# The third projection group of a Fourier branch: both differences taken ahead of the last shift on VectorE, both sums by accumulating transfers

## The chip, the core and the metric

The kernel runs on one core of a Trainium2 chip. The core has five engines, each of which runs its own list of instructions strictly in order: TensorE (PE, matmuls; PEld is its weight load), VectorE (DVE), ScalarE (ACT), GpSimd (POOL) and SyncE (SP), which here only issues transfers. Transfers between device memory and the on-chip memory run on 16 DMA engines; GpSimd, ScalarE and SyncE can each issue them, and a transfer that adds to what is in the on-chip memory is issued by GpSimd here. Engines wait for each other by semaphores. The metric is the time of one execution on the device in microseconds (us).

## The reference, cut to what matters

The model has two layers over 256 tokens of `x` and 256 of `ctx`, all in float32. Layer 0 is a Fourier branch; the change lies in its first half:

```python
shift, scale, gate = split(silu(c) @ ada_w + ada_b, 3)
h = rmsnorm(x, g) * (1 + scale) + shift
u, z = split(h @ w_in, 2)                  # w_in: 2048 x 8192, u: 256 x 4096
ug = u.reshape(b, n, 16, 256)              # 16 groups of 256 channels
f = fft2(ug, axes=(tokens, channels), norm='ortho').real
f = einsum('bngc,gcd->bngd', f, w_mix)     # one 256 x 256 mix per group
x = x + gate * ((f * silu(z)) @ w_out)
```

The same is done for `ctx` with its own shift and scale. Layer 1 is an attention branch, and a last norm ends the model.

## The kernel before, in words

The kernel takes the transform over tokens first: it multiplies the normed inputs by a cosine and sine matrix (the DFT units), so that what is projected, `hx`, is already transformed: 16 blocks (k) of 128 features, each with 256 positions for `x` and 256 for `ctx`. Scale acts on all positions, the shift only on position 0. The transform over channels is then folded into the weights: of a group's 256 columns of `w_in`, columns c and 256 - c enter as their difference (called m) and their sum (called p); the two columns that have no partner (0 and 128) of all groups form one small special product (`asp`). So each group needs, of its weight columns, one difference and one sum for each half (kh = 0, 1) of the 2048 features.

Every float32 product is made of three matmuls: an operand is split into a high part, rounded by ScalarE (line 60), and a low part, subtracted by VectorE (line 61); TensorE runs high x high, high x low and low x high (lines 73 to 75).

The work goes through these stages. (1) An opening of 16 steps (`opening_step`): SyncE loads weights of scale and shift (`ada_tile`), TensorE multiplies them, ScalarE copies the rows (`ada_rows`), TensorE turns them and VectorE reduces them (`ada_fin`, lines 222 to 225). Then `scale_hx` scales four blocks of `hx` into high and low parts (lines 276 and 277), and `fix_f0` adds the shift to their position 0 (lines 229 to 235). Steps alternate: scale of four blocks, then shift of the same four; the last `ada_fin` and `fix_f0(3)`, behind the loop, are the last shift. Projection matmuls of groups 0 and 1 fill TensorE between (`fill_pe`). (2) The other groups, g = 2 to 15: for each group TensorE runs the m product (48 matmuls, both halves), the mix of the group before (`mix`, 14 matmuls, ends in VectorE's sums `ft`, lines 504 and 505, which GpSimd writes out, line 509), the p product (48), and `load_m`'s product that turns the next mix weights into `pqh`, `pql` and `sp` (10). (3) The z part, the output product and layer 1.

A group's weights come in two loads of 1016 KB, one for each half, into the pool `raw` of three buffers (line 34), issued by SyncE (line 46). `fold_uh` makes of each the difference (line 122, into a tile `wm` of the pool `ws`) and, for g of 2 or more, the sum in place in the raw buffer: for half 0 by VectorE (line 128), for half 1 by a transfer that GpSimd issues (line 131), which fetches the second columns again from device memory and adds them to the first ones there. It has to wait until the difference is taken, since it overwrites an operand. `split_uh` makes high and low parts of both (`wmh`, `wml`, `wph`, `wpl`), into a pool of eight tiles; the raw buffer is free when `wpl` is made.

A planner puts the instructions of each engine into one order, by its own estimate of when each can run. `tc.issue_after(x)` adds that the instructions within, as far as they are on the same engine as x, stand behind x in that order. In the kernel before, group 2's folding and splitting stands within such a block in the loop over g (lines 432 to 437): half 0 behind the last shift (`f0_end`), half 1 behind the low part of the special product (`asp_end`). Its loads stand in SyncE's queue behind the last weights of the opening.

Of the kernel before, what the change touches and what calls it, by code (L numbers as in the profile page):

```python
# [10 lines left out]
F32 = mybir.dt.float32  # L11
F32R = mybir.dt.float32r
AF = mybir.ActivationFunctionType
ALU = mybir.AluOpType
# [14 lines left out]
def tile_dit(ctx: ExitStack, tc: tile.TileContext, a: dict, out: bass.AP):  # L29
    nc = tc.nc  # L30
    V, S, PE, GP = nc.vector, nc.scalar, nc.tensor, nc.gpsimd
# [70 lines left out]
    gs0 = const.tile([P, KT, 2], F32, name="gs0")  # L102
# [11 lines left out]
    GP.memset(c32, 0.0)  # L114
    V.tensor_copy(c32[:, :, 0:2], cc)

    def load_uh(g, kh, ld=raw, *until):
        return ld(a["wu"][g, kh], *until)[:, : 8 * 2 * 127].rearrange("p (k s c) -> p k s c", k=8, s=2)

    def fold_uh(v, g, kh):  # L120
        m = wsp.tile([P, 8, 127], F32, tag="ws", name="wm")
        V.tensor_tensor(m, v[:, :, 0, :], v[:, :, 1, :], op=ALU.subtract)
        if g < 2:
            t = wsp.tile([P, 8, 127], F32, tag="ws", name="wp")
            V.tensor_tensor(t, v[:, :, 0, :], v[:, :, 1, :], op=ALU.add)
            return t, m
        if kh == 0:
            V.tensor_tensor(v[:, :, 0, :], v[:, :, 0, :], v[:, :, 1, :], op=ALU.add)
        else:
            b = a["wu"][g, kh].rearrange("p (k s c) -> p k s c", k=8, s=2)[:, :, 1, :]  # L130
            nc.gpsimd.dma_start(out=v[:, :, 0, :], in_=b, accum_op=ALU.add)
        return v[:, :, 0, :], m

    def split_uh(v, m):
        fl = {}
        for nm, t in (("m", m), ("p", v)):
            l = wfp.tile([P, 8, 127], F32R, tag="wf", name=f"w{nm}l")
            h = wfp.tile([P, 8, 127], F32R, tag="wf", name=f"w{nm}h")
            split(h, l, t)
            fl[nm] = (h, l)  # L140
        return fl
# [14 lines left out]
    with tc.tile_pool(name="st", reuse_waits="tile", bufs=1, side="right") as st:  # L156
# [40 lines left out]
        f0_end = [None]  # L197
# [16 lines left out]
        def ada_fin(nb, which, rows):  # L214
            o2 = psum()
            with pe_next():
                for j in range(4):
                    r = PE.transpose(o2[:, j * P : (j + 1) * P], rows[:, j * P : (j + 1) * P], ident)
            pe_end[0] = r.ins
            kq = slice(nb * 4, nb * 4 + 4)  # L220
            dst = (sh0, gs0)[which][:, kq, :]
            V.tensor_reduce(dst, o2.rearrange("p (a j s) -> p a s j", a=4, j=4)[:, :, 0:2, :], axis=AX.X, op=ALU.add)
            V.tensor_tensor(dst, dst, adab[:, 0, which, kq], op=ALU.add)
            if which:
                V.scalar_tensor_tensor(dst, dst, 1.0, ng[:, 0, kq], op0=ALU.add, op1=ALU.mult)
# [38 lines left out]
        def evac_dft(k):  # L264
# [3 lines left out]
            V.tensor_copy(f0[:, k, :], o[:, 0::N])  # L268
            hx.append(r)

        def scale_hx(k):
            r = hx[k]
            h, l = act(F32R), act(F32R)
            for s in range(2):
                q = slice(s * N, (s + 1) * N)
                S.activation(h[:, q], r[:, q], AF.Copy, scale=gs0[:, k, s : s + 1])
                V.scalar_tensor_tensor(l[:, q], r[:, q], gs0[:, k, s : s + 1], h[:, q].bitcast(F32), op0=ALU.mult, op1=ALU.subtract)
            hx[k] = (h.rearrange("p (s j) -> p s j", s=2), l.rearrange("p (s j) -> p s j", s=2))

        raws, pend = {}, []  # L280
# [116 lines left out]
        for p in range(8, 16):  # L397
# [18 lines left out]
            for kh, q in ((0, 9), (1, 11)):  # L416
                if p == q:
                    raws[kh, 1] = fold_uh(raws[kh, 1], kh, 1)
                if p == q + 1:
                    with tc.issue_after(rows_end[0]):  # L420
                        wu[kh][1] = split_uh(*raws[kh, 1])
        ada_fin(*pend.pop())
        fix_f0(3)
        fill_pe(len(fill))

# [4 lines left out]
    asp = up.tile([96, 2, 130], F32R, name="asp", bufs=1)  # L430
    for g in range(G):
        if g == 2:
            v = [load_uh(g, kh) for kh in range(2)]
            w = []
            for kh in range(2):
                with tc.issue_after((f0_end[0], asp_end)[kh]):
                    w.append(split_uh(*fold_uh(v[kh], g, kh)))
        else:
            w = load_u(g) if g > 1 else wu[g]
        if g == 0:  # L440
# [33 lines left out]
        if g == 0:  # L474
# [4 lines left out]
            asp_end = V.tensor_tensor(asp[32:64], ov, asp[0:32].bitcast(F32), op=ALU.subtract).ins  # L479
# [73 lines left out]
    with tc.tile_pool(name="yp", reuse_waits="tile", bufs=32) as ypool:  # L553
# [20 lines left out]
        with tc.tile_pool(name="zp", reuse_waits="tile", bufs=2) as zp:  # L574
# [10 lines left out]
            for kg in range(4):  # L585
                wr = raw(a["wz0"][kg])
                w = []
# [5 lines left out]
                for j in range(4):  # L593
                    k = kg * 4 + j
                    wh, wl = w[j // 2]
                    for b in range(4):
                        q = slice((j % 2) * 512 + b * P, (j % 2) * 512 + (b + 1) * P)
# [6 lines left out]
            for b in range(4, NB):  # L604
                w = ws_split(raw(a["wz"][b - 4]))
# [3 lines left out]
                for k in range(KT):  # L609
                    wh, wl = w[k // 8]  # L610
                    q = slice((k % 8) * P, (k % 8 + 1) * P)
# [29 lines left out]
        for i in range(32):  # L641
# [3 lines left out]
            w = ws_split(raw(a["wo0"][sw, kg]))  # L645
# [10 lines left out]
            for j, b in [(j, b) for b in range(8) for j in range(2)] if edge else [(j, b) for j in range(2) for b in range(8)]:  # L656
                q = slice(b * P, (b + 1) * P)
# [53 lines left out]
    with tc.tile_pool(name="h1", reuse_waits="tile", bufs=16) as h1p:  # L711
        hx1 = []
        v2 = [[None] * 2 for _ in range(4)]
        kT = []
        with tc.tile_pool(name="kvp", reuse_waits="tile", bufs=2) as kvp:
            hc1 = []
            for k in range(KT):
# [3 lines left out]
                for s, h in ((0, hx), (1, hc)):  # L721
                    q = slice(s * N, (s + 1) * N)
# [6 lines left out]
            for kg in range(8):  # L729
                w = ws_split(raw(a["wkv"][kg]))  # L730
                for j in range(2):
                    k = kg * 2 + j
                    wh, wl = w[j]
                    for tb in range(4):
                        h = (hx1, hc1)[tb // 2][k]
                        c = (tb % 2) * P
                        for kv in range(2):
                            q = slice(kv * 512, (kv + 1) * 512)
# [276 lines left out]
        with tc.tile_pool(name="fin", reuse_waits="tile", bufs=1) as fp:  # L1015
# [22 lines left out]
            for k in range(12, NB, 2):  # L1038
                w = w1_next()
# [5 lines left out]
            for kg in range(16):  # L1045
                w = ws_split(raw(a["wo1b"][kg]))
                for j in range(2):
                    k = kg * 2 + j
                    wh, wl = w[j]
                    for tb in range(2):  # L1050
                        for c in range(2):
                            q = slice(c * 512, (c + 1) * 512)
# [24 lines left out]
            for kg in range(8):  # L1077
                t = raw(a["wo1c"][kg])
                if kg < 5:
                    w = [(h[:, q], l[:, q]) for h, l in ws_split(t) for q in (slice(0, 512), slice(512, 1024))]  # L1080
                else:
                    w = []
# [123 lines left out]
```

## Time and profile before

| what | us |
|---|---|
| median of three runs | 1873.78 |
| lowest and highest run | 1867.76, 1873.89 |
| the profiled execution, its own time | 1867.94 |
| its span | 1865.8 |
| TensorE busy in the span | 1817.2 |
| VectorE busy | 1390.8 |
| ScalarE busy | 953.4 |
| GpSimd busy | 175.2 |

Granted TensorE clock over the span: 0.996 of full speed. Times in the timelines count from the start of the span. The last scaling of the opening ends at 112.5 us, the last shift starts at 117.0 us, and the groups from 2 on run to about 330 us.

How to read the rows: a row of a timeline has start, duration, engine, line, operation, output and inputs by the program's names (numbers left out), shapes and count; brackets at the end give the idle time of the engine before it and what ended it. A row of the waits has who waited for whom, the total, the number of times and the longest. A row of busy time by stretch has the stretch, its length, the busy time of each engine with its instructions, the granted clock (1.00 is full), the share of DMA time and GB/s. Groups have a count, the busy time and the mean duration in ns, and the idle time before them. A `q` behind an engine's name is its instruction queue, which issues transfers.

### The profile page before, as it was taken

The numbers are of one execution on the slowest core, as the hardware profiler recorded it, in microseconds if no ns is written. First come the engines' busy times: TensorE is split into PE (matmuls) and PEld (weight loads), VectorE is DVE, ScalarE is ACT, GpSimd is POOL, SyncE is SP. The second block draws the span as 40 slices with busy tenths as digits, with TensorE's granted clock in tenths as the row PEclk, the third lists the DMA queues.
The fourth block names the chain that finished last, engine by engine and source line by source line (L and its number), as shares of the span: only waits on it lengthen the run. The fifth ranks groups of instructions, "written<-read, shape, count | busy, mean of one in ns | idle before, by whom it ended". The sixth has DMA issues, their size and how long they took to land.

```text
span 1865.8 us, 26461 instructions
## 1 busy us (share of the span) xinstructions
PE 1817.2 (97%) x9889; PEld 1548.6 (83%) x9889; DVE 1390.8 (75%) x2767; ACT 953.4 (51%) x1657; POOL 175.2 (9%) x188
## 2 busy tenths in 40 slices
PE   6889999999999999999999999999999999999997
PEld 4569999888888888888888787888888888887886
DVE  4658888787868788687983835788878878887455
ACT  5534444432222243324231624888888888896343
POOL 0001111200000000000000001112220220300001
PEclk9999999999999999999999999999999999999999
DMA  9978888656566547754576323333333333434543
GB/s 396 416 252 227 229 241 244 249 203 247 209 248 230 205 166 280 270 215 147 214 279 227 118 90 136 136 136 114 135 113 136 124 125 136 158 136 175 188 179 135
DMA packets 75087, 366.87 MB, mean 197 GB/s; under 512 B 22160, under 2 KB 22304, under 8 KB 39888
## 3 DMA queue, kind: packets, MB, share of 16 engines
q1 hardware_dynamic: 49104, 324.83, 47.2%
q0 software_dynamic: 21280, 32.63, 6.9%
q10 hardware_dynamic: 4576, 7.74, 1.3%
q8 instruction: 77, 1.26, 0.3%
q14 instruction: 50, 0.41, 0.1%
HBM read 352.58 MB, written 12.59 MB: 196 GB/s over the span
## 4 chain that ended last, share of the span: by engine, by line
PE 84%; DMA 7%; DVE 4%; issue 2%; ACT 2%; POOL 0%; ACTq 0%; POOLq 0%; DVEq 0%
PE ps L74 21%; PE ps L73 21%; PE ps L75 21%; PE ps L905 6%; PE ps L907 3%; DMA raw<-in_wu 3%; PE ps L961 3%; DMA raw<-in_awp 3%; PE ps L976 2%; PE ps L975 2%; PE ps L941 2%; PE ps L942 1%; PE ps L206 1%; DVE wpl L61 1%; DMA dm<-in_dmat 0%
## 5 line engine op out<-in xcount | busy, mean ns | idle before, releaser
L60 ACT CAST wh<-raw 128x1024 fp32r<-128x1024 f32 x333 | 349.5, 1051 | 556.7 <-PE ps L74 491.0
L61 DVE TENSOR_TENSOR wl<-raw,wh 128x1024 fp32r<-128x1024 f32 x333 | 421.1, 1267 | 261.1 <-ACT wh L60 258.9
L74 PE MATMUL ps<-act,wh 128*128 128x512 f32 x1024 | 398.2, 389 | 0.0
L73 PE MATMUL ps<-act,wh 128*128 128x512 f32 x1024 | 393.7, 389 | 0.0
L75 PE MATMUL ps<-act,wl 128*128 128x512 f32 x1024 | 391.2, 389 | 0.0
L75 PEld LDWEIGHTS ps<-act,wl 128*128 128x128 f32 x1024 | 192.3, 188 | 39.9
L74 PEld LDWEIGHTS ps<-act,wh 128*128 128x128 f32 x1024 | 192.3, 188 | 39.8
L73 PEld LDWEIGHTS ps<-act,wh 128*128 128x128 f32 x1024 | 192.3, 188 | 39.7
L905 PE MATMUL ps<-h,wh 128*128 128x512 f32 x512 | 186.8, 400 | 0.0
L540 DVE CUSTOM_DVE_ANT_0 raw<-raw,cb 128x512 f32<-128x512 f32 x256 | 172.4, 687 | 15.2 <-DMA raw<-in_adw 11.1
L540 DVE CUSTOM_DVE_ANT_0 junk<-raw,cb 128x512 f32<-128x512 f32 x192 | 131.6, 685 | 11.9 <-ACT cb L532 8.4
L907 PE MATMUL ps<-h,wl 128*128 128x256 f32 x512 | 138.1, 280 | 0.0
L74 PE MATMUL ps<-wl,h 128*128 128x512 f32 x320 | 125.6, 392 | 1.5 <-DVE wl L61 1.5
L73 PE MATMUL ps<-wh,h 128*128 128x512 f32 x320 | 124.4, 397 | 0.2 <-ACT h L724 0.2
L75 PE MATMUL ps<-wh,h 128*128 128x512 f32 x320 | 124.4, 391 | 0.0
L905 PEld LDWEIGHTS ps<-h,wh 128*128 128x128 f32 x512 | 96.1, 188 | 18.8
L943 DVE CUSTOM_DVE_ANT_0 ps<-ps,mask,nsink 128x512 f32<-128x512 f32 x128 | 92.0, 753 | 11.9 <-PE ps L942 10.8
L946 ACT ACTIVATE p<-ps,mx 128x512 f32<-128x512 f32 x128 | 87.2, 687 | 24.7 <-DVE mx L943 24.1
L907 PEld LDWEIGHTS ps<-h,wl 128*128 128x128 f32 x512 | 96.8, 189 | 1.4
L61 DVE TENSOR_TENSOR pl<-ps,ph 128x512 fp32r<-128x512 f32 x128 | 83.6, 684 | 10.0 <-ACT ph L60 9.1
L951 ACT ACTIVATE p<-p,sm 128x512 f32<-128x512 f32 x128 | 85.4, 716 | 7.8 <-DVE sm L949 7.8
L74 PE MATMUL ps<-wl,ys 128*128 128x512 f32 x212 | 83.3, 393 | 0.0
(311 smaller groups left out, 3565.8 us busy)
## 6 DMA issues: line engine op xcount, KB each, us to landing
raw<-in_wz SPq DMA_DIRECT2D x64, 1024.0 KB, 4.9
raw<-in_adw SPq DMA_DIRECT2D x64, 1024.0 KB, 4.9
raw<-in_awp SPq DMA_DIRECT2D x32, 1024.0 KB, 13.6
raw<-in_wo SPq DMA_DIRECT2D x32, 1024.0 KB, 5.5
raw<-in_wq SPq DMA_DIRECT2D x32, 1024.0 KB, 4.9
raw<-in_wu SPq DMA_DIRECT2D x32, 1016.0 KB, 7.3
raw<-in_wo1b SPq DMA_DIRECT2D x16, 1024.0 KB, 4.8
act<-in_xT POOLq DMA_DIRECT2D x32, 256.0 KB, 5.4
```

The source lines that it names most:

```text
L60: S.copy(h, src)
L61: V.tensor_tensor(l, src, h.bitcast(F32), op=ALU.subtract)
L73: PE.matmul(o, wh, xh, start=start, stop=False)
L74: PE.matmul(o, wh, xl, start=False, stop=False)
L75: return PE.matmul(o, wl, xh, start=False, stop=stop).ins
L540: V.tensor_tensor_reduce(junk if s == 0 and i < 3 else wf, wf, cb[:, s, kq * 512 : kq * 512 + 512], 1.0, 0.0, ALU.mult, ALU.add, acc[:, i, ...
L905: PE.matmul(o[0], wh[:, q], hx1[k], start=k == 0, stop=k == KT - 1)
L907: PE.matmul(o[0][:, 0:N], wl[:, q], hx1[k][:, 0:N], start=False, stop=False)
L943: V.tensor_tensor_reduce(o, o, mask[:, tb, :], -0.125, nsink[:, i : i + 1], ALU.add, ALU.min, mx[:, tb : tb + 1])
L946: S.activation(pt[:, tb, :], so[tb], AF.Exp, bias=mx[:, tb : tb + 1], scale=-1.0, accum_out=sm[:, tb : tb + 1])
L951: S.activation(pt[:, tb, :], pt[:, tb, :], AF.Copy, scale=sm[:, tb : tb + 1])
L961: PE.transpose(o[:, (kt * 2 + tb) * P : (kt * 2 + tb + 1) * P], pt[:, tb, c : c + P], ident)
```

## The change

Group 2's loads and foldings move from the loop over g to the end of the opening. Both differences stand behind the last scaling in VectorE's order (`scale_end`), and the last `ada_fin`, with it the last shift, stands behind the second difference (`fold_end`). Both sums of group 2 are now made by accumulating transfers that GpSimd issues; from group 3 on half 0 is summed by VectorE as before. The splits of both halves stand behind the last shift, and the order behind the special product's low part is no longer asked for.

```diff
     def fold_uh(v, g, kh):
         m = wsp.tile([P, 8, 127], F32, tag="ws", name="wm")
-        V.tensor_tensor(m, v[:, :, 0, :], v[:, :, 1, :], op=ALU.subtract)
+        fold_end[0] = V.tensor_tensor(m, v[:, :, 0, :], v[:, :, 1, :], op=ALU.subtract).ins
...
-        if kh == 0:
+        if kh == 0 and g > 2:
             V.tensor_tensor(v[:, :, 0, :], v[:, :, 0, :], v[:, :, 1, :], op=ALU.add)
         else:
             b = a["wu"][g, kh].rearrange("p (k s c) -> p k s c", k=8, s=2)[:, :, 1, :]
...
-                V.scalar_tensor_tensor(l[:, q], r[:, q], gs0[:, k, s : s + 1], h[:, q].bitcast(F32), op0=ALU.mult, op1=ALU.subtract)
+                scale_end[0] = V.scalar_tensor_tensor(l[:, q], r[:, q], gs0[:, k, s : s + 1], h[:, q].bitcast(F32), op0=ALU.mult, op1=ALU.subtract).ins
...
-        ada_fin(*pend.pop())
+        v2 = [load_uh(2, kh) for kh in range(2)]
+        with tc.issue_after(scale_end[0]):
+            v2 = [fold_uh(v2[kh], 2, kh) for kh in range(2)]
+        with tc.issue_after(fold_end[0]):
+            ada_fin(*pend.pop())
         fix_f0(3)
         fill_pe(len(fill))
...
         if g == 2:
-            v = [load_uh(g, kh) for kh in range(2)]
-            w = []
-            for kh in range(2):
-                with tc.issue_after((f0_end[0], asp_end)[kh]):
-                    w.append(split_uh(*fold_uh(v[kh], g, kh)))
+            with tc.issue_after(f0_end[0]):
+                w = [split_uh(*f) for f in v2]
```

The planner's order changes with it. On VectorE the two differences stand right behind the last scaling; behind the shift follow the low first difference, the special product, the low first sum, and, ahead of group 1's mix weights and of group 3's first difference, the low second difference. On ScalarE the rounding of the first difference stands ahead of the copy of the last rows, and the rounding of the first sum ahead of that of the second difference. On GpSimd one issue more stands ahead of the writes of group 0. On TensorE eight of the ten matmuls of group 3's mix weights move into the p product of group 2; the planner's order differs in a like manner in several of the groups that follow. SyncE's order is the same.

More of the change, by code (lines that the diff above doesn't have):

```diff
@@ L115, in tile_dit @@
     V.tensor_copy(c32[:, :, 0:2], cc)
+    fold_end = [None]
     def load_uh(g, kh, ld=raw, *until):
@@ L269, in evac_dft @@
             hx.append(r)
+        scale_end = [None]
         def scale_hx(k):
```

## The prediction

> **What bounds the kernel now.** I read the page first (span, busy time, the chain), then busy time by stretch, then who TensorE waits for in the projection, then the timelines of TensorE and VectorE around the longest of those waits.
>
> ```profile
> span 1865.8 us, 26461 instructions
> PE 1817.2 (97%) x9889; PEld 1548.6 (83%) x9889; DVE 1390.8 (75%) x2767; ACT 953.4 (51%) x1657; POOL 175.2 (9%) x188
> PE 84%; DMA 7%; DVE 4%; issue 2%; ACT 2%; POOL 0%; ACTq 0%; POOLq 0%; DVEq 0%
> ```
>
> TensorE is the bound: 97% busy, 84% of the chain. A change elsewhere is worth what it takes out of TensorE's waits, at most 3% of the span, so I look for the waits near the edit.
>
> ```profile
> core 0: us, PE busy (x) PEld busy (x) DVE busy (x) ACT busy (x) POOL busy (x), PEclk, DMA share, GB/s
> 116.00:130.00 14.00, 12.96 (x107) 12.25 (x105) 12.83 (x30) 7.60 (x15) 1.51 (x1) 1.00 0.35 105
> 130.00:140.00 10.00, 7.25 (x48) 7.26 (x49) 7.43 (x11) 4.42 (x9) 1.14 (x2) 0.83 0.82 212
> 140.00:185.00 45.00, 42.79 (x353) 42.38 (x353) 37.84 (x57) 19.84 (x39) 9.28 (x10) 1.00 0.86 226
> 185.00:230.00 45.00, 44.19 (x363) 43.65 (x362) 37.86 (x55) 20.43 (x40) 7.77 (x9) 1.00 0.83 231
> 230.00:315.00 85.00, 85.00 (x707) 85.00 (x707) 74.21 (x107) 38.09 (x76) 15.08 (x18) 1.00 0.87 238
> ```
>
> The edit lies at 112 to 140 us. Before 130 VectorE is full (12.83 of 14 us); at 130 to 140 TensorE has its hole and a granted clock of 0.83; from 230 TensorE never stops, one matmul per 85.00/707 = 0.120 us. Its waits from 118 to 340 us:
>
> ```profile
> PE ps L75 <- DVE wml L61: 4.6, 2, 3.5
> PE ps L74 <- DVE apl L61: 1.9, 3, 1.1
> PE ps L499 <- DVE asp L479: 0.3, 1, 0.3
> ```
>
> The longest, 3.5 us, is for the low part of group 2's second difference. On TensorE's timeline:
>
> ```profile
> 129.00 0.28 PE L74 MATMUL ps<-act,wmh 128*127 128x256 f32 x1
> 132.75 0.52 PE L75 MATMUL ps<-act,wml 128*127 128x256 f32 x1 [3.46 <-DVE wml L61]
> ...
> 135.84 0.41 PE L74 MATMUL ps<-act,wmh 128*127 128x256 f32 x1
> ...
> 136.97 0.28 PE L73 MATMUL ps<-mh,ch 128*128 128x256 f32 x1
> ```
>
> From 129.00 to 136.97 lie 23 matmul steps: 23 x 0.120 = 2.76 us of work in 7.97, so 5.2 us lost: 3.46 waiting, the rest at the slow clock after it (132.75 to 135.84 is 15 steps of 0.206). That is the prize. VectorE at the same place:
>
> ```profile
> 116.95 0.19 DVE L222 TENSOR_REDUCE sh<-ps 128x8 f32<-128x32 f32 x1 [4.48 <-PE ps L218]
> ...
> 118.69 0.41 DVE L347 TENSOR_TENSOR mt<-m 128x256 f32<-128x256 f32 x1
> 119.03 1.21 DVE L122 TENSOR_TENSOR wm<-raw 128x1016 f32<-128x1016 f32 x1
> ...
> 121.42 1.21 DVE L128 TENSOR_TENSOR raw<-raw 128x1016 f32<-128x1016 f32 x1
> ...
> 124.12 0.42 DVE L479 TENSOR_TENSOR asp<-ps,asp 32x260 fp32r<-32x260 f32 x1
> 124.57 1.22 DVE L122 TENSOR_TENSOR wm<-raw 128x1016 f32<-128x1016 f32 x1
> ...
> 127.84 1.20 DVE L61 TENSOR_TENSOR wpl<-raw,wph 128x1016 fp32r<-128x1016 f32 x1
> ...
> 131.49 1.20 DVE L61 TENSOR_TENSOR wml<-wm,wmh 128x1016 fp32r<-128x1016 f32 x1
> ...
> 136.98 1.22 DVE L61 TENSOR_TENSOR wpl<-raw,wph 128x1016 fp32r<-128x1016 f32 x1 [2.56 <-ACT wph L60]
> ```
>
> VectorE idles 4.48 us ahead of the last shift, then runs both differences of group 2 (119.03, 124.57) and one sum (121.42) when it is late already; the awaited low part comes at 131.49.
>
> **The change, part by part.**
>
> *Two differences ahead of the shift.* They follow the last scaling, which ends 4.48 us before 116.95, at 112.47: 112.5 to 114.9 with 2 x 1.21. Cover: the idle time, 2.1 us of which stay. If it went (a late load), the shift would slip by as much. The second half's load:
>
> ```profile
> 106.59 0.33 SPq L46 DMA_DIRECT2D raw<-in_wu  x1
> ```
> ```profile
> raw<-in_wu SPq DMA_DIRECT2D x1, 1016.0 KB, 6.9
> ```
>
> It lands at 113.5; its subtraction starts at 113.7. Cost nothing. ScalarE's rounding of the first difference (about 1.05 us) now stands ahead of its copy of the last rows:
>
> ```profile
> 114.94 0.59 ACT L211 COPY rows<-ps 128x512 f32<-128x512 f32 x1 [3.00 <-PE ps L206]
> 123.19 1.06 ACT L60 CAST wph<-raw 128x1016 fp32r<-128x1016 f32 x1
> 126.01 1.05 ACT L60 CAST wmh<-wm 128x1016 fp32r<-128x1016 f32 x1
> ```
>
> From 113.7 it ends at 114.8, before the copy's 114.94: no cost, with 0.1 us to spare.
>
> *One sum off VectorE.* With the differences, 3 x 1.21 = 3.6 us leave VectorE between 118.7 and 131.5. The low part of the special row (124.12) no longer stands behind a difference and a sum, so TensorE's 0.3 us wait for it goes. The program's order also puts group 2's second low difference ahead of group 1's mix weights and group 3's first difference.
>
> *Two accumulating transfers on GpSimd.* This is the new wait: ScalarE's rounding of the first sum now follows a landing, and behind it in ScalarE's order stand a rounding for group 1, a copy for the mix and the rounding of the second difference; on VectorE, behind the low part of that sum, stand one subtraction, two output sums and the low second difference. The rows of before:
>
> ```profile
> 126.37 1.51 POOL L131 DMA_DIRECT2D raw<-in_wu  x1 [13.63 <-PE ps L75]
> ```
> ```profile
> L131 POOL DMA_DIRECT2D raw<-in_wu x14: 1478/1488/1513, 126.4 to 314.0; - x14
> ...
>   ACT wph L60: 43.1, 12
> ...
> DMA to landing us min/median/max: 8.1/12.6/13.4
> ```
> ```profile
> 135.91 1.04 ACT L60 CAST wph<-raw 128x1016 fp32r<-128x1016 f32 x1 [4.08 <-DMA raw<-in_wu]
> ```
>
> The issue at 126.37 came 0.6 us after the subtraction it waits for (124.57 + 1.22); its sum was used at 135.91, 9.5 us on. So the first sum is issued at 114.3 and lands at T0 = 122.4 to 127.7 by the shortest and longest of the fourteen. I take 9.5, T0 = 123.8, the landing nearest in time and the first of its queue after a pause, as this one is. When is it due? Prices on VectorE:
>
> ```profile
> L61 DVE TENSOR_TENSOR wpl<-raw,wph 128x1016 fp32r<-128x1016 f32 x27 | 32.7, 1210 | 5.8 <-ACT wph L60 5.8
> ...
> L504 DVE TENSOR_TENSOR ft<-ps,gsb 128x256 f32<-128x256 f32 x26 | 10.8, 414 | 0.0
> L505 DVE TENSOR_TENSOR ft<-ps,gsb 128x254 f32<-128x254 f32 x26 | 10.6, 409 | 0.0
> ...
> L122 DVE TENSOR_TENSOR wm<-raw 128x1016 f32<-128x1016 f32 x28 | 34.0, 1216 | 20.8 <-DMA raw<-in_wu 20.7
> ...
> L61 DVE TENSOR_TENSOR apl<-ps,aph 127x260 fp32r<-127x260 f32 x14 | 5.9, 420 | 0.0
> ```
>
> From T0 to the low second difference: 1.06 + 1.21 + 0.42 + 0.41 + 0.41 + 1.20 = 4.7 us. TensorE wants it one step after 129.00, less the 0.3 gained: 128.8. So T0 is due at 124.1; 123.8 leaves 0.3 us. Each us later costs one.
>
> The second sum is issued 1.5 us behind the first, in the same queue. Bounds: 115.8 + 8.1 = 123.9 if nothing shares, 123.8 + 9.5 = 133.3 if it runs only after the first; I take 115.8 + 12.6 = 128.4, the median of the fourteen, as this one shares the engines with the first. Behind it on ScalarE stand a small copy and the rounding of group 3's mix weights (0.6, like the rows' copy of that size), some 1.7 us with its own 1.05, which TensorE wants at 131.7 (136.97 less 5.2): due at 130.0. Price 0, at the far end 3.3.
>
> The Trainium skill ("SBUF — State Buffer", "SBUF: two separate sides") says that a GpSimd-issued transfer cannot write its descriptors while VectorE holds their shared port in a two-port mode, and speaks against more of them. In the trace VectorE computed all through 126.37 to 127.9, and that issue took 1.51 us like the fourteen (1.48 to 1.51). By the rule the first issue would wait for the second subtraction's end, 114.9 for 114.3, T0 = 124.4, and the sum below would be 0.3 us smaller.
>
> *Queues and buffers.* SyncE's order of loads is as before, but each waits for one of three raw buffers. Group 3's second load waited for the low first sum of group 2, that at 127.84, ended at 129.0; now 123.8 + 1.06 + 1.21 = 126.1. Group 4's first waited for the low second sum (136.98 + 1.22 = 138.2); now, behind the low second difference (128.5), a difference, two output sums and itself (1.22 + 0.41 + 0.41 + 1.21 by their rows), two mix-weight sums (0.41 each, as at 118.69) and two small ones that I put at 0.6 each, 133.8. So loads lead by 2.9 to 4.4 us, TensorE by 5.5. GpSimd's writes of group 0 come behind the second issue, long done by then. Eight matmuls of a mix-weight product (1.0 us) move behind half of group 2's sums: same number, no gain.
>
> *The sum.* 5.2 + 0.3 = 5.5 us at 130 to 137. Later waits of the list are 1.1 (the other low difference) and 1.9 (low sums of the mix), all before 230: they can vanish (+3.0) or take back up to the 2.6 us by which TensorE's lead exceeds the loads'. I take +0.5, nearer to zero. After 230 TensorE waits for nothing, so the lead holds: 6.0 us. The profiled execution took 1867.94 us, giving 1861.9. The median of the runs is 1873.78, 5.8 above that execution, and the runs spread from 1867.76 to 1873.89, as much as the gain itself. Against the median: 1873.78 - 6.0 = 1867.8. What a measurement can tell from no change is 0.5%, 9.4 us.
>
> **The rivals.**
>
> 1. *The first sum lands late and the hole returns, slower than before.* Place: ScalarE at 124, decided at T0 = 124.1, one us per us. For: twelve of the fourteen landings were waited for by ScalarE, 43.1 us in all, and 12.6 is the median. At 12.6 (T0 = 126.9) 2.8 us are lost, gain 2.7; at 13.4, 3.6 and perhaps the slow clock's 1.7, gain near 0; beyond, at 15.5 (T0 = 129.8), 5.7 + 1.7, so 2 us slower, about 1876. Against: only one load is underway at 114 to 119. The Trainium skill ("TensorE: Matmul & The Clock Gate", "What's actually happening") has the clock halve after an idle window of about 3.4 us; the 3.46 us wait with 0.206 us steps behind it agrees, and a shorter hole would not pay the 1.7.
> 2. *The loads, not TensorE, set the pace to 230.* Then the lead falls to the loads' 2.9, gain 2.9, 1870.9. For: DMA share 0.83 to 0.87. Against: no wait at all from 230 on at 0.87.
> 3. *All later waits go too*: 5.5 + 3.0 = 8.5 us, 1865.3.
> 4. *The differences do not get ahead.* If the second load landed 2.1 us later than shown, the shift and all sums behind it would slip; gain 3 or less.
> 5. *The median falls at the low end of the spread*, where one of three runs lay before: 6.0 us lower again, 1861.8.
>
> **How the numbers follow.** Forecast, gain 4.5 to 7.5 with the runs as before: 0.45. Rival 1: 0.10, half of it a loss, 0.05 of it with other slips over 0.5%. Rival 2: 0.10. Rival 3: 0.08. Rival 4: 0.02. Rival 5: 0.25. Faster by over 0.5% is rival 5 and a little of rival 3: 0.28; slower 0.05; the rest 0.67. The range reaches from rival 5 with a little of rival 3 (1860.5) to rival 1 at a small loss (1875); the forecast's own is 1865 to 1870.
>
> **What would show it.** Right: two subtractions between 112 and 115 with the shift still near 117; two issues on GpSimd at 114 and 116, landings near 124 and 128; no TensorE wait over 1 us at 125 to 140 and granted clock 1.00 there; the first mix-weight matmul behind the second differences near 131.7, not 136.97. Wrong: ScalarE's rounding of the first sum waiting past 125 with TensorE idle at 129; or new waits for low parts at 140 to 230 that add up to 5 us.

## The result and the profile after

The changed kernel takes 1864.47 us (median of 20 runs, 1859.08 to 1871.51), the kernel before beside it 1871.26 us (20 runs, 1867.76 to 1873.89): ratio 0.9966, 95% interval 0.9956 to 0.9976, a gain of 6.8 us between the medians. Three more timings of the same order of work, further down, gave 0.9960, 0.9960 and 0.9954.

The profiled execution of the changed kernel took 1861.45 us. Its page, the span and the chain:

```profile
span 1859.1 us, 26469 instructions
PE 90%; DMA 4%; DVE 3%; ACT 2%; issue 1%; POOL 0%; ACTq 0%; POOLq 0%; SPq 0%; DVEq 0%
```

The span is 6.7 us shorter, and TensorE's share of the chain has gone from 84% to 90%. Busy time by stretch, columns as before:

```profile
116.00:130.00 14.00, 14.00 (x121) 12.89 (x114) 9.22 (x26) 8.11 (x20) 2.99 (x2) 1.00 1.00 192
130.00:140.00 10.00, 10.00 (x85) 10.00 (x84) 9.94 (x16) 5.17 (x11) 2.67 (x3) 1.00 0.78 276
```

TensorE is busy through all 24 us at full clock, where it lost its 5.2 us before. Who it waits for from 140 to 340 us is down to two rows (1.1, 1.9 and 0.3 us before):

```profile
PE ps L73 <- ACT mh L60: 0.5, 1, 0.5
PE ps L74 <- DVE apl L61: 0.2, 1, 0.2
```

The opening of this execution ran 2.1 us later than that of the kernel before (the last shift starts at 119.04, not 116.95), so every time below is to be read less 2.1. VectorE, ScalarE and GpSimd around the change:

```profile
114.47 1.21 DVE L124 TENSOR_TENSOR wm<-raw 128x1016 f32<-128x1016 f32 x1
115.85 1.22 DVE L124 TENSOR_TENSOR wm<-raw 128x1016 f32<-128x1016 f32 x1 [0.17 <-DMA raw<-in_wu]
119.04 0.19 DVE L224 TENSOR_REDUCE sh<-ps 128x8 f32<-128x32 f32 x1 [1.97 <-PE ps L220]
...
127.11 1.22 DVE L61 TENSOR_TENSOR wpl<-raw,wph 128x1016 fp32r<-128x1016 f32 x1 [1.68 <-ACT wph L60]
...
129.24 1.21 DVE L61 TENSOR_TENSOR wml<-wm,wmh 128x1016 fp32r<-128x1016 f32 x1
...
136.31 0.69 DVE L61 TENSOR_TENSOR ml<-mt,mh 128x512 fp32r<-128x512 f32 x1
```
```profile
115.77 1.04 ACT L60 CAST wmh<-wm 128x1016 fp32r<-128x1016 f32 x1 [1.73 <-DVE wm L124]
117.03 0.59 ACT L213 COPY rows<-ps 128x512 f32<-128x512 f32 x1 [0.22 <-PE ps L208]
...
126.03 1.05 ACT L60 CAST wph<-raw 128x1016 fp32r<-128x1016 f32 x1 [1.04 <-DMA raw<-in_wu]
```
```profile
116.26 2.99 POOL L133 DMA_DIRECT2D raw<-in_wu  x2 [1.44 <-PE ps L208]
```
```profile
130.62 0.28 PE L75 MATMUL ps<-act,wml 128*127 128x256 f32 x1
...
133.23 0.28 PE L73 MATMUL ps<-mh,ch 128*128 128x256 f32 x1
```

TensorE starts the last matmul of group 2's p product at 145.58 us in the kernel before, 28.63 us behind the start of the last shift, and at 141.87 here, 22.83 us behind it:

```profile
145.58 0.29 PE L75 MATMUL ps<-act,wpl 128*127 128x260 f32 x1
```
```profile
141.87 0.29 PE L75 MATMUL ps<-act,wpl 128*127 128x260 f32 x1
```

So TensorE is 5.8 us ahead when group 2 is done. Group 3's second load, which needs a raw buffer of group 2, goes out at 129.07 us in the kernel before and at 128.36 here, 12.1 and 9.3 us behind the start of the shift:

```profile
129.07 0.33 SPq L46 DMA_DIRECT2D raw<-in_wu  x1
```
```profile
128.36 0.33 SPq L46 DMA_DIRECT2D raw<-in_wu  x1
```

Both differences stand in VectorE's idle time, and 1.97 us of it are left ahead of the shift. The first sum was issued at 116.26 and rounded from 126.03 on, 9.8 us later. The low second difference ends at 129.24 + 1.21 = 130.45, and TensorE takes it at 130.62, 0.17 us behind. The `ml` at 136.31 is the low part of the mix weights that TensorE begins at 133.23. The prediction calls them group 3's; by the code they are group 2's own (`load_m(2)`).

### The profile page after: what moved, and what is told of

Same layout as the page of the kernel before. It is cut to its first block, busy times and chain, and to the rows that moved or that the text cites. A ratio compares the mean times of both kernels' runs of the same rounds, so it can differ in the third digit from the quotient of the medians.

```text
span 1859.1 us, 26469 instructions
## 1 busy us (share of the span) xinstructions
PE 1817.6 (98%) x9889; PEld 1549.3 (83%) x9889; DVE 1389.6 (75%) x2766; ACT 954.6 (51%) x1657; POOL 176.8 (10%) x189
## 4 chain that ended last, share of the span: by engine, by line
PE 90%; DMA 4%; DVE 3%; ACT 2%; issue 1%; POOL 0%; ACTq 0%; POOLq 0%; SPq 0%; DVEq 0%
PE ps L74 23%; PE ps L73 23%; PE ps L75 23%; PE ps L910 6%; PE ps L912 3%; DMA raw<-in_awp 3%; PE ps L966 3%; PE ps L981 2%; PE ps L980 2%; PE ps L946 2%; PE ps L947 2%; DMA raw<-in_wu 1%; PE ps L208 1%; PE ps L829 0%; DVE wl L61 0%
```

## The experiments

One table first. Ratios are to the kernel before, timed beside each on the same chip. The other columns, in us, are from each run's one profiled execution. The waits are those of TensorE, added up from the rows of its view of waits. "Group 2" is the time from the start of the last shift to the last matmul of group 2's p product, "groups 3 to 15" from there to the last matmul of the last p product (at 338.0 us in the kernel before, later than the 330 given ahead of the prediction). What follows takes 1527.8 to 1529.2 us in all of them, so the runs differ in these two stretches and in the start of the last shift, 117.0 to 120.6 us.

| run | ratio, 95% interval | waits 116 to 140 | waits 140 to 340 | group 2 | groups 3 to 15 |
|---|---|---|---|---|---|
| before | 1 | 3.8 | 3.3 | 28.6 | 192.4 |
| changed kernel | 0.9966, 0.9956 to 0.9976 | 0 | 0.7 | 22.8 | 189.3 |
| again | 0.9960, 0.9948 to 0.9971 | 0 | 2.7 | 22.8 | 191.1 |
| again2 | 0.9954, 0.9941 to 0.9968 | 0 | 4.7 | 22.8 | 195.0 |
| swapped | 0.9960, 0.9949 to 0.9972 | 0 | 1.1 | 22.8 | 188.9 |
| hole_filled | 1.0003, 0.9994 to 1.0012 | 0.9 | 6.8 | 27.2 | 197.3 |
| diffs_alone | 0.9978, 0.9968 to 0.9989 | 3.2 | 2.2 | 29.0 | 191.8 |
| sum_on_vector | 0.9957, 0.9944 to 0.9969 | 1.3 | 3.4 | 24.4 | 193.1 |
| sums_alone | 0.9987, 0.9977 to 0.9998 | 4.4 | 2.0 | 29.2 | 192.3 |
| order_kept | 0.9982, 0.9972 to 0.9993 | 3.1 | 0.9 | 27.6 | 189.4 |
| low_first | 0.9980, 0.9971 to 0.9989 | 0 | 3.8 | 23.1 | 194.7 |
| order_alone | 1.0006, 0.9997 to 1.0015 | 3.8 | 4.3 | 27.1 | 195.3 |
| both | 0.9971, 0.9959 to 0.9982 | 0 | 3.5 | 23.2 | 194.5 |
| all_sums | 1.0126, 1.0111 to 1.0141 | 0 | 22.2 | 22.8 | 224.1 |

Two things stand out. All runs that take both differences ahead of the last shift gain 3.1 us or more between the medians (all_sums aside), and none of the three that leave them behind it gains more than 1.9. But what a run gains in group 2 is not what it gains in all: diffs_alone gains nothing there and 4.8 us in all, low_first 5.5 there and 3.1 in all. The one profiled execution of the kernel before took 1867.94 us, 3.3 less than its median, so a column of it is not to be taken for a mean.

### again and again2: the changed kernel twice more

> The changed kernel once more, for a second profiled execution. Theory (the hole at 129 us is gone, and what is left of the spread is the opening): TensorE never waits more than 1 us between 116 and 332 us, whatever the span; ratio to the kernel before 0.995 to 0.998. Where this span differs from 1859.1 us, the difference stands ahead of the last shift already (its first profile had it at 119.04 us). Rival (the first sum lands late in some executions): a wait of 1 to 3 us for a low part stands at 128 to 132 us and makes the difference.

> The changed kernel beside these two on the same chip, and a fourth execution with a profile. Theory: no wait of TensorE over 1 us from 116 to 230 us; ratio 0.9955 to 0.997. Rival: as before, a wait for a low part at 128 to 133 us in this execution.

No wait at all at 116 to 140 us, in either. The waits behind it differ between executions of the same program, here those of again2 from 140 to 340 us:

```profile
PE ps L74 <- DVE apl L61: 2.9, 4, 0.9
PE ps L74 <- DVE ml L61: 0.6, 1, 0.6
PE ps L73 <- ACT aph L60: 0.5, 2, 0.2
PE ps L75 <- DVE wml L61: 0.4, 1, 0.4
PE ps L73 <- ACT mh L60: 0.3, 1, 0.3
```

The four executions of this order of work took 1860.65, 1861.45, 1864.27 and 1867.93 us with 1.1, 0.7, 2.7 and 4.7 us of such waits. The last shift started at 118.73 to 119.15 in all four, so the difference does not stand ahead of it: the first theory of again was wrong there. Group 2 took 22.8 us in all four, and groups 3 to 15 from 188.9 to 195.0: the spread is made there. The rival, a first sum that lands late, was seen in none. For what follows: a difference of some 4 us in the later waits of single profiles says nothing; the medians do.

### swapped: the second half's sum issued first

```diff
-            nc.gpsimd.dma_start(out=v[:, :, 0, :], in_=b, accum_op=ALU.add)
+            if g > 2: nc.gpsimd.dma_start(out=v[:, :, 0, :], in_=b, accum_op=ALU.add)
...
-            v2 = [fold_uh(v2[kh], 2, kh) for kh in range(2)]
+            v2 = [fold_uh(v2[kh], 2, kh) for kh in range(2)]; [nc.gpsimd.dma_start(out=v2[kh][0], ...) for kh in (1, 0)]
```

> The two accumulating transfers of group 2 change places: the second half's sum is issued first, the first half's 1.5 us behind it. Theory (the first landing is due at a fixed time and each us behind it costs one): in the changed kernel the first landing was at 126.01 us and the low second difference ended at 130.45, 0.17 us ahead of TensorE. Now the first half's sum lands where the second landed, near 129.2, 3.2 us later; the wait of TensorE for the low second difference comes back with about 3.0 us, with up to 1.7 us more at a slow clock; 3.0 to 4.7 us slower than the changed kernel, ratio to the kernel before 0.998 to 0.9995. Rival (the engines between have room, or TensorE regains it later): no wait over 1 us, ratio as the changed kernel's, 0.9966. Second rival (an accumulating transfer takes the same time wherever it stands, so landing is 1.5 us later): 1.3 us slower than the changed kernel.

The edit did not do it: the planner puts the transfer that can go first ahead, and GpSimd's list is that of the changed kernel, first half first. So this is one more execution of the changed order, with its time. The price of a late first landing was not measured; only the 0.17 us of room at 130.62 speak for it.

### hole_filled: the wait of the kernel before filled with work

```diff
-                    h, l = hx[k]
+                    h, l = hx[k]; [PE.matmul(oa[nm], zw, h[:, :, c0:c1], start=False, stop=False) for _ in range(24 if g == 2 and k == 8 and nm == parts[0][0] else 0)]
```

> The kernel before, with 24 matmuls of a zero weight tile (24 x 0.120 = 2.9 us, added to the second difference's product, which they leave as it is) just ahead of the product's second half, where TensorE waits 3.46 us for the low second difference. Theory (of the 5.2 us lost there 1.7 are the slow clock behind the wait, not the wait): a wait of 0.5 to 0.8 us stays, the granted clock from 130 to 140 us is 1.00, and the kernel is 1.2 to 1.7 us faster than before: ratio 0.9991 to 0.9994. Rival (the steps of 0.206 us behind the wait come from operands that arrive late, or the time is waited for again at 180 to 230 us): no change, ratio 1.000. Second rival (the added matmuls delay what follows): slower.

`zw` is a tile of zeros. On all engines the order is that of the kernel before, with these matmuls and the copy that makes the zeros added. The clock did what the theory says: a wait of 0.62 us stays, and behind it the steps are 0.12 us.

```profile
133.17 0.39 PE L75 MATMUL ps<-act,wml 128*127 128x256 f32 x1 [0.62 <-DVE wml L61]
133.39 0.28 PE L73 MATMUL ps<-act,wmh 128*127 128x256 f32 x1
133.51 0.29 PE L74 MATMUL ps<-act,wmh 128*127 128x256 f32 x1
```

The time did not follow: 1.0003, and its interval leaves out the 1.7 us and only touches the 1.2. TensorE came out of group 2 some 1.5 us earlier than before (27.2 us for 28.6), and from 140 to 340 us it waits more:

```profile
PE ps L74 <- DVE apl L61: 5.2, 6, 1.5
PE ps L75 <- DVE wml L61: 1.2, 1, 1.2
PE ps L73 <- ACT aph L60: 0.4, 1, 0.4
```

Of these, 3.0 us come behind 230 us, where the kernel before waited 0.3, and 2.6 at 180 to 230 us (1.9 before), where the rival had them. Both lie within the spread of single executions, so the place of the loss is not shown. And the run tests less than the hole: the filling takes 2.9 us of TensorE where it waited 3.46, so only the slow clock behind the wait could be gained. Whether the 3.46 us of waiting themselves are worth their length, it can't tell.

### diffs_alone and sum_on_vector: the first sum on VectorE

```diff
             b = a["wu"][g, kh].rearrange("p (k s c) -> p k s c", k=8, s=2)[:, :, 1, :]
-            nc.gpsimd.dma_start(out=v[:, :, 0, :], in_=b, accum_op=ALU.add)
+            if g > 2 or kh: nc.gpsimd.dma_start(out=v[:, :, 0, :], in_=b, accum_op=ALU.add)
...
             with tc.issue_after(f0_end[0]):
+                V.tensor_tensor(v2[0][0], v2[0][0], v21, op=ALU.add)   # v21: the first half's second columns
                 w = [split_uh(*f) for f in v2]
```

sum_on_vector adds that the second half's split stands behind `asp_end` and group 3's folding behind the low second difference.

> Both differences of group 2 ahead of the last shift as in the changed kernel, its first sum by VectorE behind the shift, the second by a transfer. Theory (the order of the differences is the gain, who makes the first sum is not): VectorE does 1.21 us more between 119 and 130, and nothing waits for a landing; by the rows of the changed kernel (shift at 119.04, 0.42 + 0.43 + 1.22 + 1.22 + 0.75 + 0.69 + 1.22 + 0.43 + 1.21 behind the shift's 2.1) the low second difference ends near 129, 1.6 us ahead of TensorE's need: no hole, ratio 0.995 to 0.998, as the changed kernel. Rival (the sum on VectorE is what makes it late): a hole of 1.2 to 3.6 us for a low part at 129 to 136 us, ratio 0.998 or more. The planner moves the mix of group 1 behind the mix weights again, as before the change.

> Both differences ahead of the last shift, the first sum by VectorE right behind the shift, and the order held so that the special row's low part stands ahead of the low second difference and group 3's differences behind it (in diffs_alone the special row came last and TensorE waited 3.2 us for it). Theory (who makes the first sum does not matter once nothing that TensorE wants stands behind it): the special row is 0.4 us late, the low second difference ends 2 us ahead of need, no wait over 1 us; the changed kernel's time within 1.5 us, ratio 0.9953 to 0.9972. Rival (taking the sum off VectorE is part of the gain): a wait of 1.2 us or more for a low part at 126 to 140 us, ratio 0.9973 or more.

In diffs_alone the planner put the special row's low part behind the second half's and a difference of group 3, and TensorE waited for that:

```profile
PE ps L504 <- DVE asp L484: 3.2, 1, 3.2
```

Neither theory had named that wait. A slow clock follows it (0.82 granted from 130 to 140 us), and group 2 takes 29.0 us, no less than before; yet 4.8 us are gained, and the ratio, 0.9978, lies inside the theory's range. With the special row moved forward the wait is 1.3 us (0.4 were expected), no slow clock follows, and the ratio is 0.9957, the changed kernel's (again2, beside it: 0.9954). So the rival's wait came, but not its loss: who makes the first sum does not show in the time, as long as nothing that TensorE wants next stands behind it.

### sums_alone: the differences left where they were

```diff
-        if kh == 0:
+        if kh == 0 and g > 2:
             V.tensor_tensor(v[:, :, 0, :], v[:, :, 0, :], v[:, :, 1, :], op=ALU.add)
```

> The kernel before, but the first sum of group 2 by a transfer that GpSimd issues, as the second; both differences stay behind the last shift. Theory (the differences' place is the gain, and a sum by a transfer pays only if it is issued early): the first difference is taken at 119 us, its sum issued at about 120.8 and landed 9.5 us later at 130.3; behind it stand 1.06 + 1.21 + 1.21 until the low second difference at 133.8, where TensorE wants it at 128.9: the hole grows from 3.5 to about 5 us, 1 to 3 us slower than before, ratio 1.0005 to 1.0016. Rival (the 1.21 us taken off VectorE are the gain): hole 2.2 us or less, 1.2 to 3 us faster, ratio 0.998 to 0.9994. The planner takes the three differences of groups 2 and 3 one after the other here.

```profile
132.12 0.39 PE L73 MATMUL ps<-act,wmh 128*127 128x256 f32 x1 [1.01 <-ACT wmh L60]
136.00 0.55 PE L75 MATMUL ps<-act,wml 128*127 128x256 f32 x1 [3.38 <-DVE wml L61]
```

The hole stays and is 4.4 us in two waits, near the theory's 5, and group 2 takes 0.6 us longer than before. Yet the kernel is 1.9 us faster between the medians, not 1 to 3 slower: the rival's time, without the rival's shorter hole. What VectorE no longer does is gained behind group 2, if at all: by the interval, 0.4 to 4.3 us.

### order_kept, low_first, order_alone and both: TensorE's later order

In the changed kernel the planner also moved matmuls: eight of the ten of group 2's mix weights behind 31 of the p product, and in groups 3 to 7 eight of the ten behind 6 to 40 matmuls of the m product instead of ahead of it. order_kept holds the old order:

```diff
-            pqh, pql, sp = load_m(g)
+            with after_("p"): pqh, pql, sp = load_m(g)        # behind the p product of the group before
...
-            m_end = part(parts[:1])
+            with after_("s") if g > 2 else nullcontext(): m_end = part(parts[:1])   # behind the mix weights
...
-            mix()
+            with after_("m"): mix()
...
-            part(parts[1:])
+            with after_("x"): ends["p"] = part(parts[1:])     # behind the mix
```

> The changed kernel with TensorE's order from group 2 on held to that of the kernel before (all ten matmuls of a mix weight, then the whole m product, then the mix, then the p product). VectorE's order at group 2 is that of the changed kernel, and differs only behind it. Theory A (the hole at 129 us and its slow clock are the gain, as forecast, and the planner's other order of groups 3 to 7 is worth nothing): no wait over 1 us at 125 to 140 us and a gain of 5.5 to 6 us, ratio 0.9965 to 0.9972. Theory B (behind the hole VectorE and the loads set the pace until some 230 us; the changed kernel's loads were ahead by only 1.6 to 5 us at groups 3 and 4, by 7 from group 5 on, and that came from the other order): the hole is gone too, but waits for low parts come back at 140 to 230 us, 2 to 4 us in all, and the gain is 2 to 4.5 us, ratio 0.9976 to 0.999.

The gain is 4.0 us between the medians, as theory B says, but not for its reason: the later waits are small, and one wait of 3.1 us with a slow clock behind it stands at 133, for the low part of group 2's mix weights. So group 2 takes 27.6 us, and nearly all of its lead is gone.

```profile
132.85 0.28 PE L359 MATMUL ps<-mh,ch 128*96 128x256 f32 x1
136.23 0.58 PE L74 MATMUL ps<-ml,ch 128*128 128x256 f32 x1 [3.10 <-DVE ml L61]
136.61 0.41 PE L75 MATMUL ps<-mh,cl 128*128 128x256 f32 x1
```
```profile
130.94 0.62 ACT L60 CAST mh<-mt 128x512 fp32r<-128x512 f32 x1 [1.07 <-DVE mt L351]
```
```profile
134.36 1.21 DVE L124 TENSOR_TENSOR wm<-raw 128x1016 f32<-128x1016 f32 x1
135.49 0.68 DVE L61 TENSOR_TENSOR ml<-mt,mh 128x512 fp32r<-128x512 f32 x1
```

Its operand is rounded at 130.94 + 0.62 = 131.56, but it stands in VectorE's order until 135.49. In the changed kernel it was as late (136.31), and the eight matmuls that wait for it had been moved behind it. low_first keeps the old order on TensorE and moves that low part forward on VectorE:

```diff
-                w = [split_uh(*f) for f in v2]
+                w = [split_uh(*v2[0]), split_uh(*v2[1], "m")]
...
+                with tc.issue_after(ends["l"]): split_uh(*v2[1], "p", w[1])   # ends["l"]: low part of the mix weights
...
-            w = load_u(g) if g > 1 else wu[g]
+            with tc.issue_after(ends["l"]) if g == 3 else nullcontext(): w = load_u(g) if g > 1 else wu[g]
```

> As the run order_kept (TensorE's order from group 2 on held to that of the kernel before), but on VectorE the low part of group 2's mix weights stands ahead of the low part of the second sum and of both differences of group 3. Theory (in order_kept the hole of 129 us had only moved: TensorE waited 3.1 us at 133 for that low part, whose rounded operand was ready at 131.56 but which ended at 136.1, behind a difference, a special row, two output sums, a low part and another difference): it now ends near 132.6, ahead of the 132.97 at which TensorE wants it; no wait over 1 us and clock 1.00 at 116 to 140 us; the 3 to 4 us that order_kept lacked come back, ratio 0.9955 to 0.997. Rival (the loads, now later by the two differences behind it, set the pace): the wait goes, but waits of 2 us or more in all come at 140 to 230 us, ratio 0.9975 to 0.999.

```profile
134.21 0.28 PE L359 MATMUL ps<-mh,ch 128*96 128x256 f32 x1
134.47 0.38 PE L74 MATMUL ps<-ml,ch 128*128 128x256 f32 x1
```

The wait is gone, no other stands at 116 to 140 us, and the clock is 1.00 there. Group 2 takes 23.1 us, 4.5 less than in order_kept. The ratio has not moved: 0.9980 against 0.9982. In its execution 3.8 us of waits come behind 140 us, which is the rival's case; by again2 such waits vary as much from one execution to the next, so it is the ratio that carries this. So the lead that TensorE won in group 2 is lost again behind it. Why is not shown: the move also puts group 3's first difference 3.3 us later, counted from the shift (135.45 us in low_first, 130.83 in order_kept), and behind group 2 VectorE's order differs from that of the changed kernel in both runs.

order_alone leaves group 2 as before the change and moves only the mix weights of groups 3 to 14; both does the same to the changed kernel:

```diff
-        elif g > 2:
-            pqh, pql, sp = load_m(g)
...
-            m_end = part(parts[:1])
-            if g == 2:
-                with tc.issue_after(f0_end[0]), tc.issue_after(m_end):
-                    pqh, pql, sp = load_m(g)
+            m_end = part(parts[:1], range(9 if g > 2 else KT))
+            with tc.issue_after(f0_end[0]), tc.issue_after(m_end): pqh, pql, sp = load_m(g)
+            if g > 2: part(parts[:1], range(9, KT))
         elif g == G - 1:
+            pqh, pql, sp = load_m(g)
```

> The kernel before, with nothing of group 2 changed, but the ten matmuls of the mix weights of groups 3 to 14 behind the 27th matmul of that group's m product instead of ahead of its first: an order much like the one that the planner took for groups 3 to 7 of the changed kernel. Theory A (the hole is the gain): the wait of 3.5 us for the low second difference stays, and at most the later waits of 3.0 us go: ratio 0.9984 to 1.000. Theory B (the loads set the pace behind the hole and the order lets them get ahead): the wait of 3.5 us stays, loads from group 5 on are issued 3 to 7 us earlier, all waits at 140 to 230 us go, and the gain is 2 to 3 us, ratio 0.9984 to 0.9989. If the order is the whole of the gain: 0.996 to 0.997.

> The changed kernel, with the later order of the run order_alone written out: from group 3 to 14 the ten matmuls of a mix weight behind the 27th of the m product. Group 2's work stands as in the changed kernel. Alone, the later order gained nothing (1.0006), and the earlier group 2 under the old later order gained 0.998 (order_kept, low_first). Theory (the two only pay together: the earlier group 2 gives VectorE and the loads a lead, and an order that does not ask for the mix weights first keeps it): the whole gain of the changed kernel, ratio 0.995 to 0.997, and the waits from 140 to 230 us add up to 2.5 us at most. Rival (it is the planner's own order of groups 3 to 7 in all its details): ratio 0.9975 to 0.999, with 3 us or more of waits from 140 to 230 us.

The later order alone gains nothing (1.0006). With the early group 2 it gives 0.9971, between the old order's 0.998 and the changed kernel's 0.996, and its interval holds both: just above the theory's range in the ratio, and 3.3 us of waits from 140 to 230 us, more than it allows. It does not decide.

### all_sums: every first sum by a transfer

```diff
-        if kh == 0 and g > 2:
+        if False:
```

> The changed kernel with the first sums of all groups from 2 on by accumulating transfers: 13 more of them, and 13 x 1.21 us less on VectorE. Theory (DMA engines are near their limit from 140 us on): in the kernel before their share was 0.87 at 14.2 us a group, 12.3 us of work; at the rate of the opening's loads (about 410 GB/s at a share of 1.0) the bytes of a group would take 8.2 us, so an accumulating transfer of 508 KB costs up to 1.24 + 4.1 us, 2.5 at the least. One more for each group makes 14.8 to 17.6 us against TensorE's 14.2: the loads set the pace, share 0.97 to 1.0, 7 to 41 us slower than the changed kernel. Rival (TensorE stays the bound, and VectorE's freed time or the GpSimd queue's room covers it): within 2 us of the changed kernel, share up to 0.95.

1895.42 us, ratio 1.0126 (1.0111 to 1.0141), 31 us slower than the changed kernel.

```profile
140.00:230.00 90.00, 80.49 (x636) 79.22 (x635) 61.70 (x92) 37.65 (x72) 21.65 (x22) 0.96 0.98 233
230.00:315.00 85.00, 73.92 (x593) 72.84 (x593) 54.94 (x84) 33.55 (x64) 20.55 (x20) 0.98 0.99 232
```

VectorE is less busy (54.94 of 85 us, 74.21 before), TensorE waits 22.2 us from 140 to 340 us (3.3 before), and the DMA share is 0.98 to 0.99. The theory holds: one accumulating transfer more per group makes the DMA engines the bound. One more in all costs nothing that the timings show (sum_on_vector does without it and is no faster).

## Why the prediction was right, and where it was not

**The sum.** A gain of 6.0 us was forecast; 6.8, 7.5, 8.4 and 7.3 us were measured between the medians. The forecast time, 1867.8, is 3.3 us above the median found. 2.5 of them are the base: the three runs shown had a median of 1873.78, the twenty 1871.26. 0.8 are the gain. Rival 5 foresaw that the spread is as large as the gain.

**Differences ahead of the shift.** Right, nearly to the row: two subtractions end 1.97 us ahead of the shift (2.1 forecast), the second waits 0.17 us for its load, and ScalarE's rounding leaves 0.22 us ahead of the copy of the rows (0.1).

**First landing.** Right: 9.8 us after the issue (9.5), used at 126.03 - 2.09 = 123.9 where 123.8 was forecast and 124.1 was due; 0.17 us of room were left of the 0.3. Rival 1 stayed close and did not come.

**Second landing.** Its rounding began at 129.56 without a wait, 127.5 by the clock of before, inside the bounds and earlier than 128.4.

**The rule on the shared port.** Misread. The Trainium skill ("SBUF — State Buffer", "SBUF: two separate sides") speaks of a VectorE operation in a two-port mode; one with two inputs on the chip, as this subtraction is, it counts only against a GpSimd operation that reads there. So the section gives no ground to hold the first issue until the second subtraction ends. The trace agrees: the issue began at 116.26, while that ran (115.85 to 117.07), and the two issues took 2.99 us together, 1.5 each.

**The hole as the prize, 5.2 us.** Half right. The hole went as forecast, the chain of the forecast describes it, and group 2 was done 5.8 us earlier in all four executions (5.5 forecast). But that this lead holds to the end and is the gain is not what the runs show. low_first has 5.5 us of it and gains 3.1; diffs_alone has none and gains 4.8; order_kept has 1.0 and gains 4.0. What the gaining runs have in common is that both differences are done ahead of the shift. With them the raw buffers come free earlier: group 3's second load is issued 6.8 to 9.7 us behind the start of the shift in these runs, 12.1 to 15.2 in the kernel before and the three runs that leave the differences behind it. The forecast had that lead (2.9 us; from 12.1 to 9.3 it is 2.8), but booked TensorE's. That the earlier loads are what carries the gain is likely and not shown. Rival 2 named a pace that is not TensorE's, with the loads as the cause, and gave it 0.10; with the old order on TensorE it is near the truth: 3.1 to 4.0 us gained, where it put 2.9. Whether the loads or VectorE's own queue hold it was not told apart. (One row was miscounted: from 132.75 to 135.84 lie 14 steps of 0.22 us, not 15 of 0.206; the 5.2 us lost do not rest on it.)

**"Eight matmuls of a mix-weight product move: same number, no gain."** Wrong. This is the step that failed. The count is the same, but TensorE would have met the low part of the mix weights 3.1 us before it was there (order_kept). The forecast asked what is late next and looked at the rounding for the mix weights, due at 130.0 and in time; it did not follow their low part through VectorE's order, behind a difference, a part of `sp`, two output sums, a low part and another difference. That the order changed in several of the later groups too was written down and not priced. With the old order 3.1 to 4.0 us are gained, with the planner's 6.8 to 8.4. How much of this is TensorE's order and how much VectorE's behind group 2 stays open. So the number came out by luck in part: a lead counted in full to the end and an order priced at nothing are two errors of opposite sign.

**Later waits, +0.5 us.** In four executions 0.7, 1.1, 2.7 and 4.7 us against 3.3 in the one of before: 1.0 less in the mean, where 0.5 were forecast. With a spread of 4 us that is no test of the size, and rival 3 (all of them gone) is nearly what the first profile alone would have said.

**One sum off VectorE.** Not needed: sum_on_vector has the whole gain without it.

## What to carry to other kernels

A wait on the bound engine is worth its length only if the next things it needs also come earlier: take the wait away in a run of its own and time that (low_first), before its length is booked as gain. Filling it with idle work is a weaker test, as only the slow clock behind it can be won. Where one program's executions differ by several us, take the time at fixed points of the program, and see in which stretch they differ. Where a planner orders the work, compare the order of all stages behind an edit, and follow every operand of a moved group through the queue of the engine that makes it, not only the one that was waited for. Put early what the engine's idle time can take, and prefer a cheap instruction there to one more accumulating transfer where the DMA share is near 0.9.

## What the runs showed of the hardware

The clock behind a wait does not go by the wait's length alone. In order_kept, with a wait of 3.10 us, the granted clock (third column from the end) was 0.83 from 130 to 140 us:

```profile
130.00:140.00 10.00, 6.90 (x46) 6.67 (x45) 9.95 (x17) 3.87 (x8) 2.67 (x3) 0.83 0.84 273
```

In order_alone a wait of 3.47 us was followed by steps of 0.12 us, full speed:

```profile
136.38 0.39 PE L75 MATMUL ps<-act,wml 128*127 128x256 f32 x1 [3.47 <-DVE wml L61]
136.60 0.28 PE L73 MATMUL ps<-act,wmh 128*127 128x256 f32 x1
136.72 0.28 PE L74 MATMUL ps<-act,wmh 128*127 128x256 f32 x1
```

In all_sums a wait of 2.13 us was followed by steps of 0.21 us until 264.1, while one of 2.65 us in the same execution was followed by steps of 0.12:

```profile
260.98 0.58 PE L73 MATMUL ps<-mh,ch 128*128 128x256 f32 x1 [2.13 <-ACT mh L60]
261.37 0.41 PE L359 MATMUL ps<-mh,ch 128*96 128x256 f32 x1
261.58 0.42 PE L73 MATMUL ps<-act,wmh 128*127 128x256 f32 x1
```

And the slow steps need not start right behind the wait: in low_first they began 1.4 us after a wait of 1.73 us had ended:

```profile
183.63 0.39 PE L74 MATMUL ps<-apl,pqh 127*128 127x260 f32 x1 [1.73 <-DVE apl L61]
...
185.39 0.42 PE L74 MATMUL ps<-act,wph 128*127 128x260 f32 x1
185.61 0.42 PE L75 MATMUL ps<-act,wpl 128*127 128x260 f32 x1
```

The Trainium skill ("TensorE: Matmul & The Clock Gate", "What's actually happening") has the clock halve after an idle window of some 3.4 us that runs freely. A window that runs freely agrees with the 3.47 us that cost no clock; if the window must be idle throughout, 2.13 and 3.10 us that did cost it do not agree. The prediction took from this rule that a shorter hole would not pay the slow clock: the runs show that it can.
